# Where the bonus operand of a RWKV-7 head group is made, and in which order key, receptance and value streams run

## The chip, the cores and the metric

The kernel runs on one core of one Trainium2 chip. The metric is the device time of one execution in microseconds (us). The kernel before took 2336.88 us, the median of 3 runs (2333.94 to 2343.57). A change of over 0.5%, some 12 us, counts as faster or slower.

## The reference, cut to what matters

One encoder layer: a half-step SwiGLU FFN, a mixer, a second half-step FFN, each between RMS norms. The mixer projects the normed input once and splits the columns: eight dilated-attention heads (q, k, v) and eight RWKV-7 heads (r, k, v and three low-rank streams). RWKV-7 runs a delta-rule scan forward and backward, adds both, normalises per head, and adds a bonus:

```python
k_dir = k[:, :, None, :] * (1.0 + (a - 1.0) * k_a)          # one per direction d
...
y = ys[:, :, 0] + jnp.flip(ys[:, :, 1], axis=1)
y = ((y - mu) * lax.rsqrt(var + GN_EPS)).reshape(B, S, C) * lnx_w + lnx_b
bonus = jnp.einsum('bshn,bsdhn,hn->bsh', r, k_dir, r_k) / N_DIRS
y = y + (bonus[..., None] * v).reshape(B, S, C)
return y * g
```

All sizes here: 1024 tokens, width 1024, 8 + 8 heads of 64, FFN 2816, everything in float32, one layer.

## The kernel before, in words

Everything is traced once, in `run`, in five stages. The tile framework derives all waits. It also sets the order on each engine: program order is a priority, and an instruction that its plan holds ready is taken ahead of an earlier one that is not. On the chip each engine, and each DMA queue (SP's, ACT's, POOL's), then runs its list strictly in that order, so one late operand holds what is queued behind it.

- **FFN1** and the low-rank streams, which leave the in-context rates `a` of both directions in DRAM (`lr_d["a"]`, one 128x1024 tile for each of four pairs of heads; the backward one stored time-reversed).
- **Attention** (`attention`, heads h = 0 to 7). Beside head h one RWKV stream is projected (`project_rwkv`, L499): its weights are loaded on SP as eight 128x128 tiles `zraw`, split into two parts by ACT and VectorE (`zh`, `zl`, 16 buffers each, two streams' worth), and 48 matmuls of 128x512 on TensorE (L514) make 128 channels by 1024 tokens; `shift` (L521) mixes neighbours in time. Stream numbers: 0 to 3 are receptance (r), 4 to 7 key (k), 8 to 11 value (v), each for one pair of heads. Stream 0 is made before the attention; beside it run `streams = [4, 5, 6, 7, 1, 2, 3]` (L1269), none beside head 7. `stream` (L570) finishes them: an r stream is stored to `rk_d[ct]` (L580); a k stream is normalised (L586 to L602) and stored to `rk_d[4 + i]`, then for each direction the rate tile `ra` is turned into the directional key (`rb`, L610 ACT, L611 VectorE), stored to `ak_d[d][4 + i]`, and into `ra` times the normalised key (L613), stored to `ak_d[d][i]` (L614). These stores go through POOL's queue.
- **Scan entry.** `prep(n)` (L803) loads 128 tokens of rates, keys and receptance for both directions and forms the chunk matrices `lm`; `solve(n)` (L863) inverts them by 62 small dependent VectorE instructions (L879, L881) after a round trip of `X` through DRAM, ending with a transpose (L883). Between the two first of these the value streams are made: 8 and 9 after `prep(0)`/`solve(0)`, 10 and 11 after `prep(1)`/`solve(1)` (L1279 to L1282). A v stream is stored to `v_d` (L617), turned (L619 to L627) and written to `vt_d` on SP (L629).
- **Scan.** `merge(n)` and `chain(n)` for n = 0 to 7, with `prep(n + 3)` and `solve(n + 3)` issued behind `chain(n)`: three block buffers go round. The buffers of `merge` lie where the projection input `x` was, so it comes after the last value stream. `chain(0)` needs all four value streams, through `uv` and `sv` (L915).
- **Finish** (`finish_unit`, L982): eight units, each two pairs of heads by 256 tokens, with three sets of buffers. Each loads on SP the scan outputs `y0`, `y1`, the directional keys `k0`, `k1`, `r`, `v` (256 KB each) and `sg` (128 KB). POOL adds `y1` reversed to `y0` (L1001) and `k1` reversed to `k0` (L1004); VectorE multiplies by `r_k` and `r` (L1006, twice); TensorE centres y (L1002), sums squares (L1011), sums the bonus over a head (L1018), turns back the scale (L1021) and makes the gate (L1032); ACT and VectorE finish (L1003 to L1035, the gate product being L1033). Then `out_project` (L1093) adds the attention half `hp`, whose loads stand on SP behind those of all units, `post` adds the residual, and **FFN2** follows.

Of the kernel before, what the change touches and what calls it, by code (L numbers as in the profile page):

```python
# [10 lines left out]
F32 = mybir.dt.float32  # L11
F32R = mybir.dt.float32r
AF = mybir.ActivationFunctionType
OP = mybir.AluOpType
# [4 lines left out]
S, D, DFF, INW = 1024, 1024, 2816, 3456  # L19
# [144 lines left out]
class _Kernel:  # L164
# [334 lines left out]
    def project_rwkv(self, p, psum, x, blocks, wide=None):  # L499

        nc, V, A, T = self.nc, self.nc.vector, self.nc.scalar, self.nc.tensor
        for c0, n in blocks:
            for d in range(2) if 4 <= c0 < 8 else ():
                a = wide.tile([128, S], F32, name="ra", tag="ra")
                self.load(a, self.lr_d["a"][d][c0 - 4])
                self.rates.append(a)
            hl = self.columns(p, ATT + c0 * 128, n * 128)
            for ct in range(c0, c0 + n):
                cs = slice((ct - c0) * 128, (ct - c0 + 1) * 128)
                ps = [psum.tile([128, 512], F32, name="zr", tag="d", bufs=2) for half in range(2)]  # L510
                for half in range(2):
                    for k, (h, l) in enumerate(hl):
                        for i, (w, j) in enumerate(((h, 0), (h, 1), (l, 0))):
                            T.matmul(ps[half], w[:, cs], x[half][j][:, k, :], start=(k == 0 and i == 0),  # L514
                                     stop=(k == NK - 1 and i == 2))
# [54 lines left out]
    def stream(self, p, psum, ct, y):  # L570

        nc, V, A, G, T = self.nc, self.nc.vector, self.nc.scalar, self.nc.gpsimd, self.nc.tensor
        if ct == 12:
            A.activation(y, y, AF.Tanh)
        elif ct == 14:
            A.activation(y, y, AF.Tanh, scale=0.5)
            V.tensor_scalar(y, y, 0.5, 0.5, op0=OP.mult, op1=OP.add)
            self.nc.gpsimd.dma_start(self.sg_d, y)
        elif ct < 4:
            self.nc.gpsimd.dma_start(self.rk_d[ct], y)  # L580
        elif ct < 8:
            i = ct - 4
            sq = p.tile([128, S], F32, name="ksq", tag="u", bufs=1)
            kr = p.tile([128, S], F32, name="kr", tag="kr", bufs=1)
            g = self.kkc[:, i:i + 1]
            A.activation(sq, y, AF.Square, scale=g)  # L586

            vs = psum.tile([128, NT, 2], F32, name="kn", tag="t")
            for t in range(NT):
                T.matmul(vs[:, t, :], sq[:, t * 128:(t + 1) * 128], self.ones2[:, ::64], start=True, stop=True)  # L590
            rs = p.tile([128, 2 * NT], F32, name="krs", tag="krs")
            A.activation(rs, vs.rearrange("p a b -> p (a b)"), AF.Sqrt)
            V.tensor_scalar(rs, rs, 1e-12, None, op0=OP.max)
            V.reciprocal(rs, rs)
            A.activation(sq.rearrange("p (a c) -> p a c", c=64), rs[:, :, None].to_broadcast([128, 2 * NT, 64]), AF.Copy)
            for half in range(2):
                q = psum.tile([128, 512], F32, name="kt", tag="t")
                for t in range(4):
                    o = half * 512 + t * 128
                    T.transpose(q[:, t * 128:(t + 1) * 128], sq[:, o:o + 128], self.ident)  # L600
                o = slice(half * 512, half * 512 + 512)
                V.scalar_tensor_tensor(kr[:, o], y[:, o], g, q, op0=OP.mult, op1=OP.mult)  # L602
            self.nc.gpsimd.dma_start(self.rk_d[4 + i], kr)
            for d in range(2):
                a = self.rates.pop(0)
                turned = lambda z: z[:, ::-1] if d else z
                for half in range(2):
                    sl = slice(half * 512, half * 512 + 512)
                    b = p.tile([128, 512], F32, name="rb", tag="vts")
                    A.activation(b, a[:, sl], AF.Identity, scale=self.kah[:, i:i + 1], bias=self.ka1[:, i:i + 1])  # L610
                    V.tensor_tensor(b, b, turned(y)[:, sl], op=OP.mult)  # L611
                    self.nc.gpsimd.dma_start(self.ak_d[d][4 + i][:, sl], b)
                V.scalar_tensor_tensor(a, a, 1.0, turned(kr), op0=OP.add, op1=OP.mult)  # L613
                self.nc.gpsimd.dma_start(self.ak_d[d][i], a)  # L614
        else:
            i = ct - 8
            self.nc.gpsimd.dma_start(self.v_d[i], y)  # L617
            back = p.tile([128, S], F32, name="vrev", tag="us")
            V.tensor_copy(back, y[:, ::-1])  # L619
            for src, dst in ((y, self.vt_d[0]), (back, self.vt_d[1])):  # L620
                for g in range(2):
                    q = psum.tile([128, 4, 128], F32, name="vt", tag="t")
                    for j in range(4):
                        t = g * 4 + j
                        T.transpose(q[:, j, :], src[:, t * 128:(t + 1) * 128], self.ident)
                    vt = p.tile([128, 4, 2, 64], F32, name="vts", tag="vts")
                    A.activation(vt.rearrange("p a b c -> p a (b c)"), q, AF.Copy)  # L627
                    for par in range(2):
                        self.nc.sync.dma_start(dst[g * 512:(g + 1) * 512, par, i, :].rearrange("(j p) c -> p j c", p=128),  # L629
                                          vt[:, :, par])  # L630
# [351 lines left out]
    def finish_unit(self, p, psum, b, g, x, g2w):  # L982

        nc, V, A, G, T = self.nc, self.nc.vector, self.nc.scalar, self.nc.gpsimd, self.nc.tensor
# [2 lines left out]
        ps2, ts = slice(2 * g, 2 * g + 2), slice(b * FB, (b + 1) * FB)  # L987
        back = slice(S - (b + 1) * FB, S - b * FB)
        z = {}
        for nm, src, sl in (("y0", self.y_d[0], ts), ("y1", self.y_d[1], back), ("k0", self.ak_d[0][4:], ts),  # L990
                            ("k1", self.ak_d[1][4:], back), ("r", self.rk_d, ts), ("v", self.v_d, ts)):
            z[nm] = p.tile([128, 2, FB], F32, name="f_" + nm, tag="f_" + nm)
            self.load(z[nm], src[ps2, :, sl].rearrange("a p t -> p a t"))
        sg = p.tile([128, FB], F32, name="f_sg", tag="f_sg")
        self.load(sg, self.sg_d[:, ts])
        y, sq, k, v = z["y0"], z["y1"], z["k0"], z["v"]
        flat = lambda q: q.rearrange("p a t -> p (a t)")
        bank = lambda nm: psum.tile([128, 2, FB], F32, name=nm, tag="d")

# [1 line left out]
        G.tensor_tensor(y, y, z["y1"][:, :, ::-1], op=OP.add)  # L1001
        T.matmul(yc, self.cen, y, start=True, stop=True)  # L1002
        A.activation(sq, yc, AF.Square)  # L1003
        G.tensor_tensor(k, k, z["k1"][:, :, ::-1], op=OP.add)  # L1004
        for j in range(2):
            V.scalar_tensor_tensor(k[:, j, :], k[:, j, :], self.rkc[:, 2 * g + j:2 * g + j + 1], z["r"][:, j, :],  # L1006
                                   op0=OP.mult, op1=OP.mult)

        vs = psum.tile([128, 4, 2], F32, name="var", tag="d")
        for u in range(4):  # L1010
            T.matmul(vs[:, u, :], flat(sq)[:, u * 128:(u + 1) * 128], self.ones2[:, ::64], start=True, stop=True)  # L1011
# [12 lines left out]
        for j in range(2):  # L1024
            i = 2 * g + j
# [80 lines left out]
    def constants(self):  # L1106
# [19 lines left out]
        self.q_d, self.kt_d = self.dram("q", [4, 128, S]), self.dram("kt", [4, 128, S])  # L1126
        self.vt_d = self.dram("vt", [2, S, 2, 4, 64])
        self.ak_d = [self.dram(f"ak{d}", [8, 128, S]) for d in range(2)]
        self.y_d = [self.dram(f"y{d}", [4, 128, S]) for d in range(2)]
        self.x_d = [self.dram(f"x{j}", [64, 1024]) for j in range(4)]  # L1130

    def mix_columns(self):
# [10 lines left out]
        self.aog = self.column("attn_out_g", 4)  # L1143
        self.rkc = p.tile([128, 4], F32, name="rkc")
        nc.gpsimd.dma_start(self.rkc, io["rwkv_r_k"].rearrange("o (a b) c -> (b c) (o a)", b=2))
        self.w0h, self.a0h = p.tile([128, 2, 4], F32, name="w0h"), p.tile([128, 2, 4], F32, name="a0h")
        for t, nm in ((self.w0h, "rwkv_w0"), (self.a0h, "rwkv_a0")):
            nc.gpsimd.dma_start(t, io[nm].rearrange("o d (k p) -> p (o d) k", p=128))
# [25 lines left out]
    def run(self):  # L1174
# [4 lines left out]
        natural = list(range(NT))  # L1179
        with self.top as top:  # L1180

            self.pool(top, "edge", side="right").tile([128, 120], F32, name="edge")
            self.constants()
            s_xn = ExitStack()
            xp = self.pool(s_xn, "xn")
# [80 lines left out]
            self.load(self.bias12, self.io["k_bias12"])  # L1266
            NB, s_sr, s_pr, s_zr, s_pm = NC_ // BLK, ExitStack(), ExitStack(), ExitStack(), ExitStack()
            zr, pz = self.pool(s_zr, "zr", 2), self.pool(s_zr, "ps_r", 1, space=PSUM)
            streams, self.rates = [4, 5, 6, 7, 1, 2, 3], []  # L1269
            self.attention(pa, wa, lambda h: self.project_rwkv(zr, pz, x, [(ct, 1) for ct in streams[h:h + 1]], wa))  # L1270
            s_at.close()
            s_pa.close()
# [3 lines left out]
            R0, R1 = (self.pool(s_sr, f"blk{j}", 1, **R) for j in range(2))  # L1276
            self.scan_constants(sp)
            blk = {}
            for n, ct in ((0, 8), (1, 10)):  # L1279
                blk[n] = self.prep(n, sp, pp, (R0, R1)[n])  # L1280
                blk[n]["inv"] = self.solve(n, sp)
                self.project_rwkv(zr, pz, x, [(ct, 1), (ct + 1, 1)])  # L1282
            s_zr.close()
            s_xn.close()
            B0 = self.pool(s_sc, "blks", 1)
# [161 lines left out]
```

## Time and profile before

| | |
|---|---|
| profiled execution, whole | 2333.77 us |
| its span in the profile | 2332.0 us |
| TensorE matmul busy in the span | 2205.8 us (95%) |
| VectorE busy | 1763.1 us (76%) |
| ScalarE (ACT) busy | 1016.8 us (44%) |
| GpSimd (POOL) busy | 565.2 us (24%) |
| mean TensorE clock granted | 0.968 of full speed |

The profile is of one execution. A busy time is the sum of an engine's instruction spans; matmuls overlap each other, so a full TensorE column is not yet TensorE at its peak. In the view by windows each row has a stretch, its length, the busy time of PE (matmul), PEld (weight load), DVE (VectorE), ACT and POOL with the number of instructions, the granted clock, the share of the DMA engines in use and GB/s. In the timeline a row has start, length, engine, line, instruction, and in brackets the idle time ahead of it with what ended it. The stages by time: FFN1 and low rank to about 790, projection of q and k to 910, attention to 1190, scan entry to 1284, scan to 1559, finish to 1615, then output projection and FFN2 to the end.

### The profile page before, as it was taken

The numbers are of one execution on the slowest core, as the hardware profiler recorded it, in microseconds if no ns is written. First come the engines' busy times: TensorE is split into PE (matmuls) and PEld (weight loads), VectorE is DVE, ScalarE is ACT, GpSimd is POOL, SyncE is SP. The second block draws the span as 40 slices with busy tenths as digits, with TensorE's granted clock in tenths as the row PEclk, the third lists the DMA queues.
The fourth block names the chain that finished last, engine by engine and source line by source line (L and its number), as shares of the span: only waits on it lengthen the run. The fifth ranks groups of instructions, "written<-read, shape, count | busy, mean of one in ns | idle before, by whom it ended". The sixth has DMA issues, their size and how long they took to land. (4 is left out here: it accounts for less than half of the span.)

```text
span 2332.0 us, 41360 instructions
## 1 busy us (share of the span) xinstructions
PE 2205.8 (95%) x15556; PEld 1784.2 (77%) x15556; DVE 1763.1 (76%) x2862; ACT 1016.8 (44%) x1910; POOL 565.2 (24%) x682
## 2 busy tenths in 40 slices
PE   6999999999999998999998999988799999999997
PEld 4788888878877676778777777765578888887886
DVE  8899999975676254677668777737899999996565
ACT  4323333354577412667554554445443323235453
POOL 6243444410000010121111111122424453441000
PEclk8999999999999999999998899999899999999999
DMA  5245544486671514555257655368434454547655
GB/s 155 89 165 170 172 145 172 151 273 191 194 233 78 217 58 119 160 173 180 54 148 207 182 147 155 105 196 281 158 122 171 160 181 140 172 158 266 194 190 180
DMA packets 351965, 388.26 MB, mean 166 GB/s; under 512 B 73491, under 2 KB 256659, under 8 KB 351765
## 3 DMA queue, kind: packets, MB, share of 16 engines
q1 hardware_dynamic: 302048, 278.53, 39.3%
q0 software_dynamic: 29360, 94.44, 10.6%
q10 hardware_dynamic: 20356, 12.66, 1.8%
q8 instruction: 122, 2.00, 0.4%
q14 instruction: 79, 0.64, 0.1%
HBM read 260.68 MB, written 124.85 MB: 165 GB/s over the span
## 5 line engine op out<-in xcount | busy, mean ns | idle before, releaser
L186 ACT ACTIVATE wh<-raw 128x512 fp32r<-128x512 f32 (+1 forms) x273 | 167.9, 627 | 264.4 <-PE gu L81 97.5
L187 DVE TENSOR_TENSOR wl<-raw,wh 128x512 fp32r<-128x512 f32 (+1 forms) x273 | 278.5, 1023 | 5.2 <-ACT wh L186 4.3
L81 PE MATMUL gu<-xh,wh 128*128 128x512 f32 x704 | 277.1, 394 | 1.0 <-ACT xh L186 0.8
L81 PE MATMUL gu<-xl,wh 128*128 128x512 f32 x704 | 275.7, 392 | 0.0
L81 PE MATMUL gu<-xh,wl 128*128 128x512 f32 x704 | 275.7, 392 | 0.0
L415 PE MATMUL pd<-gl,gwh 128*128 128x512 f32 x616 | 240.4, 390 | 2.7 <-DVE gl L187 2.7
L415 PE MATMUL pd<-gh,gwh 128*128 128x512 f32 x616 | 239.5, 390 | 0.6 <-DVE row L86 0.6
L415 PE MATMUL pd<-gh,gwl 128*128 128x512 f32 x616 | 239.7, 389 | 0.0
L86 DVE TENSOR_TENSOR row<-gu,row 128x512 f32<-128x512 f32 x308 | 206.8, 684 | 24.6 <-PE gu L81 23.9
L187 DVE TENSOR_TENSOR gwl<-graw,gwh 128x512 fp32r<-128x512 f32 (+1 forms) x176 | 118.1, 674 | 128.7 <-ACT gwh L186 128.3
L116 POOL DMA_DIRECT2D d_hid<-row x154 | 84.7, 551 | 474.0 <-DVE row L114 451.1
L186 ACT ACTIVATE gwh<-graw 128x512 fp32r<-128x512 f32 (+1 forms) x176 | 101.2, 576 | 190.1 <-PE pd L415 157.4
L81 PEld LDWEIGHTS gu<-xh,wh 128*128 128x128 f32 x704 | 133.5, 190 | 30.0 <-ACT xh L186 2.0
L81 PEld LDWEIGHTS gu<-xl,wh 128*128 128x128 f32 x704 | 133.2, 189 | 27.4
L81 PEld LDWEIGHTS gu<-xh,wl 128*128 128x128 f32 x704 | 133.0, 189 | 27.5
L415 PEld LDWEIGHTS pd<-gl,gwh 128*128 128x128 f32 x616 | 115.6, 188 | 28.0 <-DVE gl L187 4.4
L415 PEld LDWEIGHTS pd<-gh,gwh 128*128 128x128 f32 x616 | 115.5, 188 | 25.6 <-DVE row L86 1.0
L415 PEld LDWEIGHTS pd<-gh,gwl 128*128 128x128 f32 x616 | 115.6, 188 | 23.7
L94 ACT ACTIVATE row<-row 128x512 f32<-128x512 f32 x44 | 27.8, 633 | 223.2 <-DVE row L86 215.6
L187 DVE TENSOR_TENSOR gl<-raw,gh 128x512 fp32r<-128x512 f32 x160 | 112.5, 715 | 15.1 <-ACT gh L186 14.9
L145 POOL TENSOR_TENSOR ws<-ws 128x512 f32<-128x512 f32 x88 | 114.3, 1299 | 1.2
L186 ACT ACTIVATE gh<-raw 128x512 fp32r<-128x512 f32 x160 | 98.0, 621 | 33.1 <-DMA raw<-in_ffn_w_down_dram 19.8
(356 smaller groups left out, 5251.5 us busy)
## 6 DMA issues: line engine op xcount, KB each, us to landing
d_hid<-row POOLq DMA_DIRECT2D x154, 256.0 KB, 2.4
graw<-d_hid SPq DMA_DIRECT2D x132, 256.0 KB, 3.1
raw<-in_ffn_w_gate_dram SPq DMA_DIRECT2D x88, 256.0 KB, 3.1
raw<-in_ffn_w_up_dram SPq DMA_DIRECT2D x88, 256.0 KB, 3.3
ws<-in_ffn_w_down_dram SPq DMA_DIRECT2D x88, 256.0 KB, 4.9
d_ws<-ws POOLq DMA_DIRECT2D x88, 256.0 KB, 2.3
raw<-d_ws SPq DMA_DIRECT2D x88, 256.0 KB, 2.7
raw<-in_ffn_w_down_dram SPq DMA_DIRECT2D x66, 256.0 KB, 3.5
```

The source lines that it names most:

```text
L81: self.K.nc.tensor.matmul(ps, a[:, k, :], b[:, k, :], start=(k == 0 and i == 0), stop=(k == 3 and i == 2))
L86: add = lambda o, x: V.tensor_tensor(o, ps, x, op=OP.add)
L94: A.activation(y[:, 0], y[:, 0], AF.Silu)
L116: put = lambda n, y: G.dma_start(self.hid[n - 1, j // 2], y)
L145: G.tensor_tensor(o, a, b, op=OP.subtract)
L186: self.nc.scalar.activation(h, src, AF.Copy)
L187: (eng or self.nc.vector).tensor_tensor(l, src, h, op=OP.subtract)
L415: T.matmul(ps[x], a[:, ts], b, start=(m == 0 and k == 0), stop=(m == NM - 1 and k == 2))
```

## The change

The bonus operand, `r_k * r * (k_dir0 + k_dir1)`, is made in `stream` at the end of each key stream, for all 1024 tokens of a pair of heads, and stored to a new DRAM tensor `fk_d`; `finish_unit` loads it as one tile. Since the sum of the two directional keys is `k * (k_a * (a0 + a1) / 2 + 2 * (1 - k_a / 2))` in the kernel's terms, it is made from the rate tiles: POOL adds them, ACT applies scale and bias with `r_k` folded in (`khr`, `k1r`, made once in `mix_columns`, kept in a padding tile that was there already), POOL multiplies r by k, VectorE multiplies both. For that a key stream loads the finished r stream from `rk_d`, so every k stream now comes after its r stream: `[4, 1, 5, 2, 6, 3, 7]`. Two more 128x1024 buffers (`rr`, `rs`) are taken. The four value streams all come after `solve(1)`.

```diff
         for c0, n in blocks:
-            for d in range(2) if 4 <= c0 < 8 else ():
-                a = wide.tile([128, S], F32, name="ra", tag="ra")
-                self.load(a, self.lr_d["a"][d][c0 - 4])
+            for tag, src in (("ra", self.lr_d["a"][0][c0 - 4]), ("ra", self.lr_d["a"][1][c0 - 4]),
+                             ("rr", self.rk_d[c0 - 4])) if 4 <= c0 < 8 else ():
+                a = wide.tile([128, S], F32, name=tag, tag=tag)
+                self.load(a, src)
                 self.rates.append(a)
+            if 4 <= c0 < 8:
+                self.rates.append(wide.tile([128, S], F32, name="rs", tag="rr"))
...
             self.nc.gpsimd.dma_start(self.rk_d[4 + i], kr)
-            for d in range(2):
-                a = self.rates.pop(0)
+            rates, r, both = self.rates[:2], *self.rates[2:]
+            self.rates.clear()
+            G.tensor_tensor(both, rates[0], rates[1][:, ::-1], op=OP.add)
+            G.tensor_tensor(r, r, y, op=OP.mult)
+            A.activation(both, both, AF.Identity, scale=self.khr[:, i:i + 1], bias=self.k1r[:, i:i + 1])
+            V.tensor_tensor(both, both, r, op=OP.mult)
+            self.nc.gpsimd.dma_start(self.fk_d[i], both)
+            for d, a in enumerate(rates):
...
-        for nm, src, sl in (("y0", self.y_d[0], ts), ("y1", self.y_d[1], back), ("k0", self.ak_d[0][4:], ts),
-                            ("k1", self.ak_d[1][4:], back), ("r", self.rk_d, ts), ("v", self.v_d, ts)):
+        for nm, src, sl in (("y0", self.y_d[0], ts), ("y1", self.y_d[1], back), ("k", self.fk_d, ts), ("v", self.v_d, ts)):
...
-        G.tensor_tensor(k, k, z["k1"][:, :, ::-1], op=OP.add)
-        for j in range(2):
-            V.scalar_tensor_tensor(k[:, j, :], k[:, j, :], self.rkc[:, 2 * g + j:2 * g + j + 1], z["r"][:, j, :],
-                                   op0=OP.mult, op1=OP.mult)
...
+        self.khr, self.k1r = self.edge[:, 0:4], self.edge[:, 4:8]
+        G.tensor_tensor(self.khr, self.kah, self.rkc, op=OP.mult)
+        G.tensor_tensor(self.k1r, self.ka1, self.rkc, op=OP.mult)
+        G.tensor_scalar(self.k1r, self.k1r, 2.0, None, op0=OP.mult)
...
-            streams, self.rates = [4, 5, 6, 7, 1, 2, 3], []
+            streams, self.rates = [4, 1, 5, 2, 6, 3, 7], []
...
-            for n, ct in ((0, 8), (1, 10)):
+            for n, cts in enumerate(([], [8, 9, 10, 11])):
                 blk[n] = self.prep(n, sp, pp, (R0, R1)[n])
                 blk[n]["inv"] = self.solve(n, sp)
-                self.project_rwkv(zr, pz, x, [(ct, 1), (ct + 1, 1)])
+                self.project_rwkv(zr, pz, x, [(ct, 1) for ct in cts])
```

More of the change, by code (lines that the diff above doesn't have):

```diff
@@ L995, in finish_unit @@
         self.load(sg, self.sg_d[:, ts])
-        y, sq, k, v = z["y0"], z["y1"], z["k0"], z["v"]
+        y, sq, k, v = z["y0"], z["y1"], z["k"], z["v"]
         flat = lambda q: q.rearrange("p a t -> p (a t)")
@@ L1128, in constants @@
         self.ak_d = [self.dram(f"ak{d}", [8, 128, S]) for d in range(2)]
+        self.fk_d = self.dram("fk", [4, 128, S])
         self.y_d = [self.dram(f"y{d}", [4, 128, S]) for d in range(2)]
@@ L1180, in run @@
         with self.top as top:
-            self.pool(top, "edge", side="right").tile([128, 120], F32, name="edge")
+            self.edge = self.pool(top, "edge", side="right").tile([128, 120], F32, name="edge")
             self.constants()
```

## The prediction

> **What bounds the kernel now.** I read the page first (which engine is full), then the view by windows over the stages that the change touches, then the waits, the chain and the timeline of the finish, last the timelines around the scan's entry. In the windows the columns behind the length are PE, PEld, DVE, ACT and POOL busy, clock, DMA share, GB/s.
>
> ```profile
> span 2332.0 us, 41360 instructions
> ```
>
> ```profile
> 940.00:1190.00 250.00, 246.66 (x2440) 197.05 (x2439) 168.29 (x448) 157.59 (x368) 47.66 (x61) 0.99 0.44 131
> 1190.00:1284.00 94.00, 83.60 (x765) 68.37 (x765) 75.97 (x207) 45.38 (x87) 12.64 (x27) 0.88 0.81 213
> 1284.00:1535.00 251.00, 230.86 (x4829) 194.31 (x4825) 177.94 (x526) 124.64 (x226) 36.90 (x69) 0.92 0.50 140
> 1535.00:1559.00 24.00, 18.94 (x347) 15.56 (x346) 4.78 (x8) 8.35 (x17) 8.78 (x8) 0.86 0.83 262
> 1559.00:1615.00 56.00, 47.30 (x192) 29.77 (x191) 41.51 (x70) 30.54 (x62) 15.12 (x12) 0.94 0.85 288
> 1615.00:1720.00 105.00, 85.89 (x409) 68.33 (x408) 87.41 (x123) 51.53 (x100) 26.53 (x18) 0.92 0.47 151
> ```
>
> The attention (first row) is TensorE's: 246.66 of 250 us, while POOL, ACT and DVE have room. The scan's entry (second row) has three full resources at once: PE 89%, DVE 81%, DMA 0.81. The finish (fifth row) is held by none of its engines alone: PE 84%, DVE 74%, DMA 0.85. What it waits for stands in the waits of 1558 to 1620 (total, times, longest) and in the chain:
>
> ```profile
> POOL f_y L1001 <- DMA f_y<-d_y: 18.3, 4, 7.2
> POOL f_k L1004 <- DMA f_k<-d_ak: 13.6, 5, 7.9
> ...
> DVE f_k L1006 <- POOL f_k L1004: 3.2, 2, 2.6
> ```
>
> ```profile
> 1582.14 4.06 DMA f_k<-d_ak
> ...
> 1591.08 6.07 DMA f_k<-d_ak
> ...
> 1597.30 1.28 POOL f_k L1004
> ```
>
> Twice the key loads stand on the chain that ended last, once with POOL's key sum behind them. Both go away with the change.
>
> **The change, part by part.**
>
> *Finish.* These rows are the operations removed, and the two that show the pace:
>
> ```profile
> L1006 DVE SCALAR_TENSOR_TENSOR f_k<-f_k,rkc,f_r x16: 445/480/1537, 1546.6 to 1604.3; 128x256 f32<-128x256 f32 x16
> ...
> L1004 POOL TENSOR_TENSOR f_k<-f_k,f_k x8: 1261/1267/1717, 1545.3 to 1602.4; 128x512 f32<-128x512 f32 x8
> ```
>
> ```profile
> f_k<-d_ak SPq DMA_DIRECT2D x16, 256.0 KB, 5.3
> ...
> f_r<-d_rk SPq DMA_DIRECT2D x8, 256.0 KB, 5.5
> ```
>
> ```profile
> L1033 DVE TENSOR_TENSOR f_y<-f_y,gate x8: 680/687/690, 1562.9 to 1613.4; 128x512 f32<-128x512 f32 x8
> ```
>
> ```profile
> 1560.76 1.02 PE L1002 MATMUL yc<-f_y,k_cen 128*128 128x512 f32 x2
> ...
> 1566.40 1.02 PE L1002 MATMUL yc<-f_y,k_cen 128*128 128x512 f32 x2
> ```
>
> Per unit go two VectorE instructions of 0.48 (0.96 us), one of POOL of 1.27, and three loads of 256 KB against one that comes. Over eight units that is 7.7 us of DVE, 10.1 of POOL and 16 x 256 KB = 4.2 MB, which at the window's 288 GB/s are 14.6 us of DMA. None of these adds up with the others; the pace tells what is gained. Now the gate product L1033 comes every (1613.4 - 1562.9) / 7 = 7.21 us. Two units that had all loads in time followed each other on PE in 1566.40 - 1560.76 = 5.64 us. **Upper end**: all seven gaps shrink to that, 7 x 1.57 = 11.0. **Lower end**: only the longest wait for POOL's sum goes, 2.6 us. DVE alone gives 7 x 0.96 = 6.7, as it is the engine in whose line the waits end. The y loads, which have the largest wait (18.3), remain, but come forward, because a third of the traffic around them is gone. I take **-7.5**, near DVE's share.
>
> What comes behind is late next: `out_project` waits for its `hp` rows, whose loads stand on SP behind those of the last unit, so it moves with the stage and I carry the gain over whole. If it does not (DVE is busy 87.41 of 105 us behind it), the gain is nothing; that is a rival.
>
> In the scan's last chain, TensorE is held by the first unit:
>
> ```profile
> 1544.65 1.22 PE L1002 MATMUL yc<-f_y,k_cen 128*128 128x512 f32 x1 [4.49 <-POOL f_y L1001]
> ```
>
> ```profile
> 1545.00:1550.00 5.00, 5.00 (x61) 3.50 (x61) 1.79 (x3) 1.08 (x2) 2.53 (x2) 0.50 1.03 335
> ```
>
> These are 4.5 us of waiting and some 2.5 more at a granted clock of 0.50. The y loads of the first unit stand ahead of its key loads on SP, so what is removed comes behind them. I cost this at nothing; at best it gains 7.0.
>
> *Attention.* A key stream adds two POOL instructions, one ACT, one DVE (all 128x1024), a load and a store of 512 KB. Nearest rows:
>
> ```profile
> L610 ACT ACTIVATE rb<-ra,ka,kah x16: 797/800/816, 928.9 to 1083.8; 128x512 f32<-128x512 f32 x16
> ```
>
> ```profile
> L613 DVE SCALAR_TENSOR_TENSOR ra<-ra,kr x8: 1215/1221/1224, 982.9 to 1088.7; 128x1024 f32<-128x1024 f32 x8
> ...
> L614 POOL DMA_DIRECT2D d_ak<-ra x8: 532/541/548, 984.4 to 1090.3; - x8
> ```
>
> ```profile
> L586 ACT ACTIVATE ksq<-us,c_rwkv_k_k x4: 1151/1151/1152, 970.2 to 1076.3; 128x1024 f32<-128x1024 f32 x4
> ```
>
> POOL: no row of this size; L1004 does half of it in 1.27, so 2.5 each (1.27 to twice the slowest, 3.4), 20 us for four streams. ACT: between L586's 1.15 and twice L610's 0.80, say 1.4, together 5.6. DVE: 1.2 as L613, together 4.9. All fit into what the first row leaves free (POOL 202, ACT 92, DVE 82 us), PE hides them, DMA is at 0.44. Cost nothing; if a head's softmax chain stood behind POOL's two instructions, at most 5 us in each of four heads, 20. On POOL's queue the directional-key stores and the head's own sums come behind the new ones, nobody else. The `rr` load stands on SP ahead of the weights: for stream 4 it waits for stream 0, made just before, 0 to 4 us at the start; I take 0. The three small instructions in `mix_columns` run on an idle POOL.
>
> Alternation puts a **key stream last**, and `prep(0)` needs its stores:
>
> ```profile
> 1172.58 0.59 POOL L580 DMA_DIRECT2D d_rk<-us  x1 [8.46 <-issue]
> ```
>
> ```profile
> 1192.82 0.50 SPq L182 DMA_DIRECT2D ka<-d_ak  x1
> ```
>
> ```profile
> DMA to landing us min/median/max: 2.3/2.5/2.8
> ```
>
> (The last row is that of the `rb` stores.) A key stream took 1090.3 - 1076.3 = 14.0 us from its square to its last store, plus 1.4 and 1.2 for the new ones in between, plus 2.5 to land. From 1172.6, where the last stream is done now, this ends at 1191.7; the load is issued at 1192.8. So the slack is one us. Bounds 0 and +5; I take **+1.5**.
>
> *Entry.* Value streams are the bulk of PE's work here, and `chain(0)` needs them all:
>
> ```profile
> L514 PE MATMUL zr<-xh,zl x61: 387/389/497, 1186.1 to 1255.4; 128*128 128x512 f32 x61
> ```
>
> ```profile
> 1238.11 0.29 DVE L881 TENSOR_TENSOR Ti<-Ti,ttmp 128x136 f32<-128x136 f32 x1
> 1238.32 0.29 DVE L187 TENSOR_TENSOR zl<-zraw,zh 128x128 fp32r<-128x128 f32 x1
> 1238.52 0.29 DVE L879 TENSOR_TENSOR ttmp<-X,Ti 128x128 f32<-128x128 f32 x1
> ```
>
> ```profile
> 1218.60 3.63 SPq L629 DMA_DIRECT2D d_vt<-vts  x3
> 1222.27 0.54 SPq L182 DMA_DIRECT2D kd<-d_ak  x1
> ```
>
> ```profile
> 1191.16 0.39 PE L514 MATMUL zr<-xh,zh 128*128 128x512 f32 x1
> 1191.38 0.39 PE L514 MATMUL zr<-xl,zh 128*128 128x512 f32 x1
> ```
>
> Today value splits slip in between two steps of a solve (second fence), so a lower place need not hold them up: I expect streams 8 and 9 where they are, 10 and 11 a little later, and `prep(1)` up to 3.6 us earlier, because stores of values no longer stand ahead of its `kd` load (third fence). Bounds: -4, and on the other side streams 10 and 11 running only after `solve(1)`, when TensorE has nothing else: 2 x 48 matmuls, one every 0.23 us (last fence), 22 us. I take **+1**, nearest to the row that shows the splits slipping in.
>
> **Sum**: -7.5 + 1.5 + 1 = -5, so 2333.77 - 5 = 2329 for an execution like the profiled one, which lies 3.1 under the median of 2336.88 of runs 9.6 apart. From the median the same sum gives 2332. I say **2330**.
>
> *A rule against it.* DVE and POOL disturb each other in this trace:
>
> ```profile
> 1550.11 1.54 DVE L1006 SCALAR_TENSOR_TENSOR f_k<-f_k,rkc,f_r 128x256 f32<-128x256 f32 x1
> ```
>
> ```profile
> 1550.10 1.27 POOL L1004 TENSOR_TENSOR f_k<-f_k,f_k 128x512 f32<-128x512 f32 x1 [0.16 <-DMA f_k<-d_ak]
> ```
>
> Beside POOL's sum the instruction took 1.54 instead of 0.45. The Trainium skill, "SBUF — State Buffer", section "Who interferes with whom", says that a VectorE instruction with two SBUF inputs and a GpSimd one that reads SBUF exclude each other for a whole instruction; the row agrees. By that rule each new POOL instruction can stop DVE for its length.
>
> **The rivals.**
>
> 1. *More than forecast.* The lighter burst also frees the last chain's 7.0 us, the finish reaches 5.64 a unit (-11.0), and `prep(1)`'s 3.6 count: 2333.8 - 11.0 - 7.0 - 3.6 + 1.5 = 2314 at most; with half of `prep(1)`'s part and 9.5 of the finish, **2317**. For it: DMA ran at 335 GB/s in that burst. Against: the held matmul waits for y, not k. 0.20.
> 2. *Slower: values starve.* DVE serves both solves before any split of streams 10 and 11, TensorE stands still, and `merge(0)` too, whose buffers wait for the last value matmul. It decides as soon as `solve(1)` has its X before stream 10 is split. Price 22: 2333.8 - 7.5 + 1.5 + 22 = **2350**; with one stream late, 2339. For it: DVE is 81% busy there, and the entry has no other bulk work for PE. Against: the slipping in. 0.16.
> 3. *The gain is absorbed* behind the finish, by the DVE work of 1615 to 1720: 2333.8 + 2.5 = **2336**. Against: the row loads of that stretch stand behind the units on SP. 0.09.
> 4. *POOL stops DVE* in the attention, 8 x 2.5 = 20 us, and heads wait: 2329 + 20 = **2349**. Against: 82 us of DVE are free there. 0.05.
>
> **How the numbers follow.** The forecast has 0.50, with a range of its own from 2321 to 2338. A measurement of this kernel tells 0.5%, 12 us, from no change, so faster means under 2325, slower over 2348.6. Faster: 0.18 of rival 1 and 0.10 of the forecast, 0.28. Slower: 0.09 of rival 2 and 0.03 of rival 4, 0.12. The rest, 0.60, is within. The range of 8 in 10 goes from 2314, the far end of rival 1, to 2347, which leaves out the worse halves of rivals 2 and 4.
>
> **What would show it.** Right: L1033 every 6 to 6.3 us, no wait for `f_k` on the chain, the last value matmul before 1260, `ka` issued by 1196, head intervals in the attention unchanged in sum. Wrong: a stretch between 1230 and 1290 in which PE has no `zr` matmul while L879 and L881 run back to back; a finish that still takes 7 us a unit because y is late; or a first load of `prep(0)` after 1198.

## The result, and the profile after

The changed kernel took 2325.51 us, the median of 20 runs (2318.77 to 2336.66), against 2335.56 of the kernel before (20 runs, 2328.55 to 2343.57). The ratio of the runs is 0.9965, 95% interval 0.9952 to 0.9977: 8.2 us faster (5.4 to 11.2), which is within the 0.5% that counts as no change; the two medians differ by 10.1. The forecast was 2330, from a sum of -5.

Of the profile after, first the span and the windows that the prediction showed of before. Columns behind the length: PE, PEld, DVE, ACT, POOL busy, clock, DMA share, GB/s.

```profile
span 2329.8 us, 41363 instructions
```

```profile
940.00:1190.00 250.00, 244.18 (x2353) 195.22 (x2350) 177.56 (x435) 158.01 (x365) 61.58 (x66) 0.97 0.48 142
1190.00:1284.00 94.00, 83.58 (x701) 66.81 (x701) 74.52 (x207) 41.55 (x88) 14.22 (x25) 0.88 0.72 193
1284.00:1535.00 251.00, 232.08 (x4818) 196.44 (x4817) 185.01 (x546) 129.93 (x231) 38.30 (x73) 0.91 0.55 151
1535.00:1559.00 24.00, 18.23 (x374) 15.09 (x370) 4.10 (x6) 7.31 (x16) 6.91 (x10) 0.86 0.75 226
1559.00:1615.00 56.00, 53.53 (x375) 37.94 (x376) 35.07 (x59) 35.28 (x71) 8.29 (x7) 0.97 0.79 265
1615.00:1720.00 105.00, 89.62 (x408) 71.88 (x407) 88.00 (x128) 52.43 (x101) 29.08 (x19) 0.89 0.42 138
```

These stretches are fixed in time, while the scan now ends 8.4 us later, so the fifth row holds some of the scan's last matmuls. The same three parts, cut at events, are fairer: first score to first load of `prep(0)` (attention), to the scan's last output copy (entry and scan), to the last gate-up matmul of FFN2. Before, then after:

```profile
932.50:1192.10 259.60, 256.26 (x2497) 204.81 (x2496) 171.08 (x457) 161.94 (x379) 48.82 (x64) 0.98 0.45 132
1192.10:1558.90 366.80, 331.20 (x5922) 276.51 (x5921) 257.38 (x735) 176.41 (x324) 57.16 (x101) 0.91 0.60 166
1558.90:2103.40 544.50, 516.68 (x2290) 415.39 (x2289) 497.18 (x593) 198.11 (x364) 214.72 (x231) 0.98 0.52 174
```

```profile
937.60:1204.66 267.06, 260.58 (x2511) 207.85 (x2510) 188.49 (x465) 166.91 (x388) 66.78 (x73) 0.97 0.48 143
1204.66:1567.30 362.64, 327.41 (x5912) 273.69 (x5911) 254.06 (x730) 175.77 (x319) 55.79 (x101) 0.90 0.60 165
1567.30:2100.80 533.50, 515.77 (x2286) 418.38 (x2285) 487.94 (x580) 199.05 (x364) 210.29 (x226) 0.97 0.51 172
```

The attention is 7.5 us longer. TensorE stands idle in it for 6.5 us instead of 3.3, and VectorE works 17.4 us more, where four instructions of 1.2 us were to come. The other 4.3 us are TensorE's busy time (260.58 against 256.26), at a granted clock of 0.97 instead of 0.98; an estimate that scales 256.26 by these two puts 2.6 of them down to the clock. Entry and scan are 4.2 shorter, with the same idle time of TensorE (35.2 against 35.6) and a clock no higher (0.90 against 0.91); why, these rows do not show. Over the executions below this part varies by more: 359.0 us at a clock of 0.93 in order_values, 384.6 at 0.87 in order_only (different orders of streams, but the clock differs too). Behind the scan 11.0 us are gained, nearly all of it TensorE's idle time (544.50 - 516.68 = 27.8 before, 533.50 - 515.77 = 17.7 after). The attention also begins 5.1 later, so the parts give 7.5 - 4.2 - 11.0 + 5.1 = -2.6, near the two spans' -2.2. The medians differ by more, because the profiled execution after (2331.59) lies 6.1 above its median and the one before 1.8 below that of the 20.

How the 11 us come about stands in the finish: the gate product by its line, the first row add of the output projection, and SP's timeline (the DMA issues of its queue, x6 for six in a row), after; then SP's before.

```profile
L1036 DVE TENSOR_TENSOR f_y<-f_y,gate x8: 677/687/690, 1570.3 to 1619.8; 128x512 f32<-128x512 f32 x8
...
L1105 DVE TENSOR_TENSOR row<-row,pw x16: 660/677/687, 1595.4 to 1657.9; 128x512 f32<-128x512 f32 x16
```

```profile
1584.56 0.46 SPq L182 DMA_DIRECT2D row<-d_hp  x1
...
1601.53 0.47 SPq L182 DMA_DIRECT2D row<-d_hp  x1
...
1605.80 3.63 SPq L182 DMA_DIRECT2D row<-d_hp  x6
```

```profile
1599.04 4.55 SPq L182 DMA_DIRECT2D row<-d_hp  x6
...
1615.99 0.90 SPq L182 DMA_DIRECT2D row<-d_hp  x2
```

The pace of the units is hardly changed: (1619.8 - 1570.3) / 7 = 7.07 us instead of 7.21. One execution says little about so small a difference: over the runs below the unit of before has a pace of 6.67 to 7.48 us (five kernels), the light one of 7.07 to 7.26 (six). But the first rows of the output projection are now loaded among the units' loads, and the first row add comes 28.1 us after the scan's end (1567.3), where it came 51.3 after it. So most of half 0 of the output projection is done inside the finish: 76 of its 96 matmuls and five of its eight row adds come before the last gate product, where it was 35 and two. From the scan's end to the last gate product TensorE is now 96% busy (before 84%; each row is one kernel's, from 1558.90 before, from 1567.30 after):

```profile
1558.90:1613.40 54.50, 45.80 (x185) 28.45 (x184) 40.07 (x67) 29.82 (x61) 15.12 (x12) 0.94 0.86 288
```

```profile
1567.30:1619.80 52.50, 50.15 (x223) 35.08 (x222) 39.00 (x64) 33.74 (x70) 8.28 (x7) 0.97 0.88 298
```

The wait for the key sum is gone, and that for y is longer than before (waits of 1558 to 1620; total, times, longest):

```profile
POOL f_y L1009 <- DMA f_y<-d_y: 29.9, 4, 18.7
```

### The profile page after: what moved, and what is told of

The parts are those of the page before. It is cut to its first block, busy times and chain, and to the rows that moved or that the text cites. A ratio compares the mean times of both kernels' runs of the same rounds, so it can differ in the third digit from the quotient of the medians.

```text
span 2329.8 us, 41363 instructions
## 1 busy us (share of the span) xinstructions
PE 2206.4 (95%) x15556; PEld 1787.0 (77%) x15556; DVE 1767.7 (76%) x2850; ACT 1022.4 (44%) x1914; POOL 580.1 (25%) x689
## 5 line engine op out<-in xcount | busy, mean ns | idle before, releaser
L187 DVE TENSOR_TENSOR wl<-raw,wh 128x512 fp32r<-128x512 f32 (+1 forms) x273 | 278.6, 1024 | 4.1 <-ACT wh L186 2.9
L187 DVE TENSOR_TENSOR gwl<-graw,gwh 128x512 fp32r<-128x512 f32 (+1 forms) x176 | 118.0, 673 | 130.1 <-ACT gwh L186 128.4
L187 DVE TENSOR_TENSOR gl<-raw,gh 128x512 fp32r<-128x512 f32 x160 | 112.3, 713 | 15.4 <-ACT gh L186 15.0
```

The lines of the kernel that those rows point to most:

```text
L187: (eng or self.nc.vector).tensor_tensor(l, src, h, op=OP.subtract)
```

## The experiments

Two theories. **T1**, the prediction's: a lighter unit runs faster, -7.5, and the rest costs next to nothing. **T2**, formed from the traces: the units keep their pace; the gain is half 0 of the output projection inside the finish, and it is larger, but the attention and the order of streams take some of it back. All ratios are to runs of the kernel before on the same chip; the third column is the ratio's distance from 1 in us of that kernel's median. The columns behind it come from one profiled execution each. "Attention" and "behind" are the first and third of the parts above; "d_x" is the time from the first load of `prep(0)` to the second set of `d_x` stores, which release `solve(1)`; "last zr" that to the last matmul of a value stream; "idle" TensorE's in entry and scan.

| kernel | ratio (95%) | us | attention | d_x | last zr | idle | behind |
|---|---|---|---|---|---|---|---|
| before | | | 259.6 | 45.5 | 63.3 | 35.6 | 544.5 |
| changed | 0.9965 (0.9952-0.9977) | -8.2 | 267.1 | 41.5 | 63.6 | 35.2 | 533.5 |
| fin_light | 0.9947 (0.9928-0.9967) | -12.4 | 258.8 | | | 38.6 | 533.8 |
| fin_loads | 0.9956 (0.9939-0.9973) | -10.3 | 257.8 | | | 37.9 | 534.6 |
| fin_ops | 0.9984 (0.9970-0.9998) | -3.7 | 258.0 | | | 37.3 | 540.4 |
| hp_early | 1.0036 (1.0019-1.0053) | +8.4 | 257.6 | | | 35.3 | 552.5 |
| order_only | 1.0050 (1.0030-1.0070) | +11.7 | 258.3 | 55.0 | 74.2 | 46.1 | 549.3 |
| values_only | 1.0005 (0.9987-1.0023) | +1.2 | 260.2 | 36.7 | 64.5 | 39.4 | 546.9 |
| order_values | 0.9982 (0.9963-1.0001) | -4.2 | 259.0 | 40.7 | 62.8 | 39.9 | 543.2 |
| order_vt_pool | 1.0005 (0.9992-1.0018) | +1.2 | 257.9 | 43.2 | 62.9 | 38.5 | 549.6 |
| bonus_order | 1.0023 (1.0002-1.0044) | +5.4 | 265.4 | 55.0 | 74.2 | 48.8 | 533.2 |
| rr_late | 0.9951 (0.9931-0.9971) | -11.5 | 263.0 | 42.8 | 64.8 | 35.2 | 534.1 |
| rr_late_dve | 0.9950 (0.9934-0.9967) | -11.7 | 261.2 | 40.6 | 61.7 | 37.3 | 532.1 |
| keep_order | 0.9979 (0.9966-0.9993) | -4.9 | 267.4 | 44.2 | 62.2 | 37.7 | 533.6 |

Without the bonus the attention takes 257.6 to 260.2 us in these executions, and with the heavy finish of before the part behind the scan 543.2 to 549.6 (hp_early aside): what is smaller than that is read from the ratios. TensorE's idle time in the attention spreads less: 2.9 to 3.5 us without the bonus, and with it 6.5 (changed), 6.9 (bonus_order), 5.9 (rr_late), 4.8 (rr_late_dve) and 7.7 (keep_order).

### The finish by itself

**fin_light**, in the kernel before:

```diff
         for nm, src, sl in (("y0", self.y_d[0], ts), ("y1", self.y_d[1], back), ("k0", self.ak_d[0][4:], ts),
-                            ("k1", self.ak_d[1][4:], back), ("r", self.rk_d, ts), ("v", self.v_d, ts)):
+                            ("v", self.v_d, ts)):
...
-        G.tensor_tensor(k, k, z["k1"][:, :, ::-1], op=OP.add)
-        for j in range(2):
-            V.scalar_tensor_tensor(k[:, j, :], k[:, j, :], self.rkc[:, 2 * g + j:2 * g + j + 1], z["r"][:, j, :],
-                                   op0=OP.mult, op1=OP.mult)
```

> The kernel before with the lighter finish alone: one key operand is loaded per unit, no second key, no r; POOL's key sum and both L1006 are left out. It leaves out the backward direction, r and r_k of the bonus. Nothing is added in the attention. Recorded reasons: the gate product every 6 to 6.3 us instead of 7.2, in all 7.5 us faster than before. Rival (the first half of the output projection is taken in among the units): the gate product still about every 7 us, the first row add some 15 us earlier against the end of the scan, from the end of the scan to the last gate-up matmul of FFN2 11 us less than the 544.5 of before, in all 9 to 13 us faster.

Measured: 12.4 us faster, the gate product every (1618.1 - 1567.3) / 7 = 7.26 us, first row add 29.5 after the scan's end instead of 51.3, 10.7 us less behind the scan. T2's numbers.

**fin_loads** has the first hunk alone, with `v` in place of `k1` and `r`; **fin_ops** the second alone.

> The kernel before with the finish's loads of the second key and of r left out, and its instructions kept: POOL adds v reversed and VectorE multiplies by v in their place, so the bonus is of other operands. Recorded reasons (pace set by VectorE's share of a unit): nothing of the 6.7 us comes, 0 to 3 faster. Rival (the row loads of the output projection come earlier on SP because 14 loads fewer stand ahead of them): most of the 11 us, 8 to 11 faster, first row add some 15 us earlier.

> The kernel before with the finish's key sum on POOL and both L1006 left out and all seven loads kept. It leaves out the backward direction, r and r_k of the bonus. Recorded reasons: most of the gain comes from VectorE's 0.96 us a unit, 5 to 7 us faster. Rival (SP's order decides): the row loads stay behind the units' loads, 0 to 4 us faster.

Measured: the loads alone bring 10.3 us, at the old pace of (1609.7 - 1559.5) / 7 = 7.17, with all of VectorE's and POOL's work in place; the instructions alone bring 3.7 (interval 0.5 to 7.0), and there the pace is (1606.7 - 1560.3) / 7 = 6.63, which over seven gaps is 4.1. The gate product and the first row add of fin_loads, then of fin_ops:

```profile
L1033 DVE TENSOR_TENSOR f_y<-f_y,gate x8: 648/686/689, 1559.5 to 1609.7; 128x512 f32<-128x512 f32 x8
...
L1102 DVE TENSOR_TENSOR row<-row,pw x16: 666/676/687, 1588.3 to 1652.3; 128x512 f32<-128x512 f32 x16
```

```profile
L1028 DVE TENSOR_TENSOR f_y<-f_y,gate x8: 681/686/689, 1560.3 to 1606.7; 128x512 f32<-128x512 f32 x8
...
L1097 DVE TENSOR_TENSOR row<-row,pw x16: 662/677/689, 1604.6 to 1652.5; 128x512 f32<-128x512 f32 x16
```

In fin_loads the row add comes 31.9 us after the scan's end (1556.4), in fin_ops it stays late, after 47.4 (1557.2). T1's mechanism may exist, then, at half its price and as long as the projection stays outside. But the profile does not prove it: order_values has the heavy unit of before and the same pace, 6.67. In fin_loads, too, less of the projection lies inside the finish than in the changed kernel (53 matmuls and four row adds before the last gate product; TensorE is busy for 45.72 of its 53.30 us, 86%), and yet the part behind the scan is 9.9 us shorter. So it is shown that the loads bring the gain; that it comes by way of the projection is read from the traces. A kernel with fewer loads and late rows, which would separate the two, was not run.

**hp_early** asks whether early rows are enough:

```diff
-            self.load(h2[t], self.hp_d[t * 128:(t + 1) * 128, :])
+            if half:
+                self.load(h2[t], self.hp_d[t * 128:(t + 1) * 128, :])
...
+            for t in self.order[:4]:
+                self.load(h2[t], self.hp_d[t * 128:(t + 1) * 128, :])
             self.finish_half(fi, pf, 1, x)
```

> The kernel before with the row loads of the output projection's first half written ahead of the second half of the finish, nothing else. SP then has the four row loads after the first unit's second load group, ahead of the loads of units 4 to 7. Recorded reasons (these loads follow the units and cost nothing themselves): no gain, or up to 5 us slower, since 2 MB go ahead of the units' loads. Rival (half 0 of the output projection waits for nothing but its rows): first row add 15 us or more earlier, 8 to 13 us faster than before with the finish as heavy as ever.

Neither: 8.4 us slower, and T2 in this form falls. In hp_early the same two lines read:

```profile
L1033 DVE TENSOR_TENSOR f_y<-f_y,gate x8: 677/686/689, 1555.1 to 1613.4; 128x512 f32<-128x512 f32 x8
...
L1103 DVE TENSOR_TENSOR row<-row,pw x16: 630/679/689, 1585.3 to 1651.2; 128x512 f32<-128x512 f32 x16
```

The row add comes early (34.2 after the scan's end), but the units take 8.33 us each on the mean, 7 x 1.12 = 7.8 more in all. Most of that is one gap of 14.4 us, from the fourth gate product (1577.0) to the fifth (1591.4), whose unit's loads the four row loads stand ahead of. Early rows by themselves do not pay; in the kernels where they do, the units have 16 loads (4.2 MB) fewer, and the changed kernel brings two rows forward, not four.

### The order of streams and the place of the value streams

```diff
-            streams, self.rates = [4, 5, 6, 7, 1, 2, 3], []
+            streams, self.rates = [4, 1, 5, 2, 6, 3, 7], []
```

is **order_only**; **values_only** is the change's last hunk alone; **bonus_order** is the changed kernel with 8, 9 and 10, 11 where they were.

> The kernel before with the stream order 4 1 5 2 6 3 7 alone; bonus and value streams as before. Recorded reasons: a key stream last ends about 1191, so `ka` of the first prep(0) is issued 0 to 5 us later (1193 to 1198) and the whole is 0 to 5 us slower, 1.5 likely. Rival, in which the 12 us by which the changed kernel enters the scan later come from the load of r ahead of the weights: the first zr matmul of stream 4 stays at 933, ka as above. Rival, in which they come from the order: ka at 1200 to 1206 and the whole 8 to 15 slower.

> The kernel before with all four value streams placed behind solve(1) alone. Recorded reasons: between 4 us faster and 22 slower, +1 likely; last value matmul 1254 to 1260. Rival: the entry costs 3 to 5 us more (the changed kernel's first solve step came 15.7 later and the first chain instruction 18 later, where its first prep load came 12.5 later), and the scan gives most of it back: 0 to 4 us in the whole.

> The changed kernel with value streams 8 and 9 behind solve(0) and 10 and 11 behind solve(1) again, as before. Recorded reasons: the finish gains 7.5 and the attention gives up 1.5, so 6 us faster than before, 1 us faster than the changed kernel. Rival (the gain comes from the output projection's first half being taken in among the units, and most of the cost lies in the attention): finish and attention as in the changed kernel, 8 to 12 us faster than before.

The order alone costs 11.7 us (interval 7.0 to 16.4; the medians differ by 8.0), the value streams alone nothing that can be told (+1.2, interval -3.0 to +5.4), and the changed kernel without its last hunk is 5.4 slower than before instead of 8.2 faster. For order_only and bonus_order none of the recorded readings held as a whole: the first load came early and the kernel was slower all the same, and bonus_order was to be 6 to 12 us faster. The key stream being last is not why: in order_only the first load of `prep(0)` is issued at 1191.27, earlier than the 1192.10 of before. What changes comes behind it on SP. In the kernel before, in order_only, then in order_values:

```profile
1199.90 0.50 SPq L182 DMA_DIRECT2D ka<-d_ak  x1
...
1209.31 0.93 SPq L629 DMA_DIRECT2D d_vt<-vts  x2
```

```profile
1203.17 0.79 SPq L182 DMA_DIRECT2D th_w<-d_w  x1
1206.19 6.41 SPq L629 DMA_DIRECT2D d_vt<-vts  x4
1212.65 0.54 SPq L182 DMA_DIRECT2D ka<-d_ak  x1
```

```profile
1199.59 4.44 SPq L182 DMA_DIRECT2D ka<-d_ak  x2
1204.09 0.50 SPq L629 DMA_DIRECT2D d_vt<-vts  x1
1205.47 0.36 SPq L182 DMA_DIRECT2D kd<-d_ak  x1
```

In order_only eight stores of value stream 8 stand ahead of `ka` of `prep(1)`, and the last four hold SP for 6.4 us; before, that load was issued at 1199.90, ahead of them all. The `d_x` stores of `solve(1)` come after 55.0 us instead of 45.5, the last value matmul after 74.2 instead of 63.3, and TensorE is idle for 46.1 us of entry and scan instead of 35.6. bonus_order has the same three numbers (55.0, 74.2, 48.8). Two runs test that.

**order_values** has both moves, no bonus. **order_vt_pool** is order_only with

```diff
-                        self.nc.sync.dma_start(dst[g * 512:(g + 1) * 512, par, i, :].rearrange("(j p) c -> p j c", p=128),
+                        self.nc.gpsimd.dma_start(dst[g * 512:(g + 1) * 512, par, i, :].rearrange("(j p) c -> p j c", p=128),
```

> The kernel before with both moves and without the bonus: stream order 4 1 5 2 6 3 7, and all value streams behind solve(1). If the two moves only add up (12 for the order, 0 for the values, as measured alone): 10 to 14 us slower than before. If they belong together (with the alternating order the stores of value stream 8 stand on SP ahead of the loads of prep(1); behind solve(1) they come after them): 0 to 4 us slower, the second set of d_x stores within 38 to 42 us of the first load of prep(0), against 55.0 with the order alone and 45.5 before.

> The kernel before with the stream order 4 1 5 2 6 3 7 and the value stores d_vt issued on POOL's queue instead of SP's. If the 12 us of the order come from those stores standing on SP ahead of the loads of prep(1): the second set of d_x stores within 46 us of the first load of prep(0) instead of 55.0, and 0 to 4 us slower than before. If they come from the key stream being last, or from what the value streams take of VectorE and TensorE: still 8 to 14 us slower.

Either cures most or all of it: -4.2 (interval -8.6 to +0.2) and +1.2 (-1.9 to +4.2) instead of +11.7, `d_x` after 40.7 and 43.2, last value matmul after 62.8 and 62.9, and TensorE's idle time 39.9 and 38.5 instead of 46.1. The two moves do not add up; the place of the value streams is the repair of what the order does to SP's queue. Whether order_values is a little faster than before is open: its interval takes in 1.

### The attention

**rr_late** loads r behind the weights of its key stream:

```diff
-                             ("rr", self.rk_d[c0 - 4])) if 4 <= c0 < 8 else ():
...
             hl = self.columns(p, ATT + c0 * 128, n * 128)
+            if 4 <= c0 < 8:
+                self.rates += [wide.tile([128, S], F32, name=q, tag="rr") for q in ("rr", "rs")]
+                self.load(self.rates[2], self.rk_d[c0 - 4])
```

> The changed kernel with the load of r placed behind the eight weight loads of its key stream instead of ahead of them. Recorded reasons (the load of r costs nothing): same time as the changed kernel within 2 us. Rival (SP stands behind that load at the head of the attention): the first zr matmul of stream 4 goes from 946.8 back to 933 to 936, the first load of prep(0) from 1204.7 to 1192 to 1197, and the whole is 4 to 10 us faster than the changed kernel, 12 to 18 faster than before.

Inconclusive. The first zr matmul is back beside the first score (931.1 and 930.3), and prep(0) is loaded 263.0 us behind the latter instead of 267.1. But the interval of its ratio overlaps that of the changed kernel, TensorE's idle time in the attention is nearly the same (5.9 against 6.5), and the rest of the difference is busy time of the same 2511 matmuls, 257.07 us at a granted clock of 0.99 against 260.58 at 0.97:

```profile
930.30:1193.31 263.01, 257.07 (x2511) 205.10 (x2510) 189.03 (x465) 167.26 (x386) 66.97 (x73) 0.99 0.49 146
```

The wait that was to go is still there. In both kernels it stands ahead of the two `ra` loads, not of `rr`. SP's waits and issues at the head of the attention, changed kernel and rr_late:

```profile
SPq L182 <- DMA d_rk<-us: 9.6, 1, 9.6
```

```profile
920.16 1.10 SPq L182 DMA_DIRECT2D kp<-d_kt  x2
930.98 0.80 SPq L182 DMA_DIRECT2D ra<-d_a  x2
931.83 0.43 SPq L182 DMA_DIRECT2D rr<-d_rk  x1
```

```profile
SPq L182 <- DMA d_rk<-us: 9.4, 1, 9.4
```

```profile
913.13 1.11 SPq L182 DMA_DIRECT2D kp<-d_kt  x2
923.73 0.80 SPq L182 DMA_DIRECT2D ra<-d_a  x2
924.58 1.85 SPq L182 DMA_DIRECT2D zraw<-in_w_in_dram  x4
```

Every kernel here that loads r for stream 4 has this wait, and no other has it. Why it stands ahead of `ra`, I have not found, so what it costs by itself was not measured. The same kernels are those that take the buffers `rr` and `rs`, so a wait for the place of a buffer is as possible as one for r; neither was tested.

VectorE shows a second cost. The changed kernel, one moment of VectorE and of POOL:

```profile
977.72 0.68 DVE L653 TENSOR_TENSOR sb<-s,n 128x512 f32<-128x512 f32 x1
978.32 2.56 DVE L620 TENSOR_TENSOR rb<-rb,us 128x512 f32<-128x512 f32 x1
980.80 1.21 DVE L612 TENSOR_TENSOR rs<-rs,rr 128x1024 f32<-128x1024 f32 x1
```

```profile
977.93 2.40 POOL L610 TENSOR_TENSOR rr<-rr,us 128x1024 f32<-128x1024 f32 x1 [6.29 <-ACT e L722]
```

`rb`, normally 0.68 us, ends 0.55 after POOL's product ends (980.88 against 980.33): it did not get through until that product was done. **rr_late_dve** puts both POOL instructions on VectorE:

```diff
-            G.tensor_tensor(both, rates[0], rates[1][:, ::-1], op=OP.add)
-            G.tensor_tensor(r, r, y, op=OP.mult)
+            V.tensor_tensor(both, rates[0], rates[1][:, ::-1], op=OP.add)
+            V.tensor_tensor(r, r, y, op=OP.mult)
```

> The changed kernel with r loaded behind the weights, and the two POOL instructions of the bonus (sum of the rates, r times k) on VectorE. If the attention's 4 to 8 us come from POOL stopping VectorE: rb (L620) back from 1.17 to 0.68 us, the weight split L187 from 0.39 to 0.31, VectorE's work in the attention 186 us against 189.0 in spite of 9.8 us taken over, first score to first load of prep(0) 259 to 261 us against 263.0, and the whole 2 to 4 us faster than with POOL. If they come from the traffic, or from what the key stream asks of VectorE itself: VectorE's work above 195, the stretch 263 us or longer, the whole not faster.

VectorE, by line and form, in rr_late and then in rr_late_dve (busy us, mean ns):

```profile
L187 DVE TENSOR_TENSOR zl<-zraw,zh 128x128 fp32r<-128x128 f32 x78 | 28.2, 390 | 6.7 <-ACT zh L186 6.0 <-ACT n L669 0.3 <-PE zr L517 0.2
L620 DVE TENSOR_TENSOR rb<-rb,us 128x512 f32<-128x512 f32 x16 | 18.5, 1173 | 0.3 <-ACT rb L619 0.2
```

```profile
L187 DVE TENSOR_TENSOR zl<-zraw,zh 128x128 fp32r<-128x128 f32 x78 | 25.3, 348 | 6.6 <-ACT zh L186 6.5
L620 DVE TENSOR_TENSOR rb<-rb,us 128x512 f32<-128x512 f32 x16 | 10.9, 684 | 0.0
```

VectorE does 9.8 us more of its own and is busy for 186.8 us instead of 189.0; the attention is 1.8 us shorter (261.2, just beyond the 259 to 261 expected; the weight split L187 comes back to 0.35 us, not to 0.31), and TensorE's idle time in it 4.8 instead of 5.9. That is somewhat less than half of the 4.0 between rr_late and order_values (259.0), which has the same order and no bonus. In the whole, where 2 to 4 us were expected, it is not to be told from rr_late.

**keep_order** makes the bonus without moving any stream: a key stream stores k times both directions to a new tensor, and the r stream that comes later loads it and multiplies.

```diff
+            if c0 in (1, 2, 3, 4):
+                self.rates.append(wide.tile([128, S], F32, name="rr", tag="rr"))
+                self.load(self.rates[-1], self.ks_d[c0] if c0 < 4 else self.rk_d[0])
...
+            if ct:
+                ks = self.rates.pop()
+                G.tensor_tensor(ks, ks, y, op=OP.mult)
+                self.nc.gpsimd.dma_start(self.fk_d[ct], ks)
...
```

> The bonus made beside the attention with the order of streams and the place of the value streams as before: a key stream stores k times both directions, the later r stream of the same heads loads it, multiplies on POOL and stores the bonus operand; only stream 4 loads the r that is there, behind its weights. If the attention's cost is that of the order (a key stream last, values later): the finish's 11 us remain whole, 9 to 12 us faster than before, first load of prep(0) at 1190 to 1194. If it is that of the bonus instructions and their traffic themselves: first load of prep(0) 4 us or more later against the first score than the 259.6 of before, and 4 to 8 us faster.

4.9 us faster, attention 267.4: the second theory. The finish's gain is whole (533.6 behind the scan), entry and scan are as before, and the attention is 7.8 us longer although no stream was moved, with 4.3 us more idle time of TensorE (7.7 against 3.3). For three of the four key streams it stores one operand more than the changed kernel does (k times both directions, 512 KB), so the two costs need not be equal.

## Why the prediction was right, and where it was not

- **Time and class** were right: 2330 forecast, 2325.5 measured, within 0.5%. The sum of -5 compares with the measured -8.2, and that it came so near was luck in good part: a gain that was too small (-7.5 for 11.0) stood beside a cost of the attention that was put at nothing.
- **Finish, -7.5**: sign right, mechanism wrong. The step that failed is "I take -7.5, near DVE's share", with the pace of 6 to 6.3 us a unit that it implied. The changed kernel has 7.07, and y comes late, which were two of the signs of being wrong. VectorE's and POOL's share alone gave 3.7 (fin_ops, 0.5 to 7.0), the loads alone 10.3 (fin_loads). The premise under it failed too: "`out_project` waits for its `hp` rows, whose loads stand on SP behind those of the last unit". That order is no constant of the kernel. It is planned anew from what else there is to load, and with fewer loads two rows go among the units. What I had called the upper end, 11.0, was reached, but not by the shorter unit that stood behind it.
- **The last chain's stall, cost 0**: nothing came of it; TensorE still waits for POOL's sum of y at the first unit, and y still arrives late.
- **Attention, cost nothing**: undersized. The idle time on VectorE and POOL was there, yet the stage lengthened by 7.5 us in the changed kernel's profile, 5.8 in bonus_order, 3.4 in rr_late, 7.8 in keep_order, at clocks of 0.97 to 0.99; TensorE's idle time in it grew by 3.1, 3.5, 2.6 and 4.3. Rival 4 had the mechanism and put 20 us on it; VectorE was in fact busy for some 12.5 more than its own new work (17.4 less the 4.9 of L612), and taking POOL out shortened the stage by 1.8. "For stream 4 it waits for stream 0 ... I take 0" was wrong as to the wait: it is 9.6 us of SP, ahead of `ra` and not of `rr`, with an end of 4 in the prediction.
- **Last key stream, +1.5**: 0. The first load of `prep(0)` comes within 1.5 us of the attention's last reduction (1190.7 and 1192.10 before, 1191.9 and 1191.27 in order_only), with the key stream last or not. The slack of one us that I had worked out was not on the path.
- **Entry, +1**: right in size (TensorE's idle time in entry and scan 35.2 against 35.6), for a reason that I had not seen. "Streams 8 and 9 where they are" holds (last value matmul 63.6 us behind the first load, 63.3 before), `prep(1)` comes 4 us earlier, as hoped. But without the last hunk the new order would have cost some 12 us, by value stores ahead of `prep(1)` on SP: the rival that was missing. Rival 2, value streams starved by both solves, did not occur.

The profile's signs: no wait for the key sum was right, though the chain that ended last goes back to 1628.64 only and so does not show the finish. The attention's length, which was to stay, grew by 7.5 us. `ka` at 1196, the first load of `prep(0)` by 1198 and the last value matmul by 1260 failed (1205.24, 1204.66, 1268.3), all three by the attention's later start and greater length and not by the entry.

## What to carry to other kernels

When loads are taken out of a stage, ask what the planner will put in their place: the gain here came without a faster unit, with TensorE less idle and most of the next stage's first half done inside the finish, and loading that work early without making the room first lost 8.4 us. Where a queue is shared, read what the new order of producers puts ahead of the next consumer's loads, since two moves that cost 12 and 0 us alone may be free together. Idle time on VectorE does not pay for new POOL work beside it: count the stops of VectorE as well, and read a stage's cost from idle time, which moved less than the stage's length did with the clock.

## What the runs showed of the hardware

A 128x1024 product of two operands took 2.39 us on POOL (L610) and 1.22 on VectorE (rr_late_dve); I had estimated 2.5 for POOL from a row half its size. A VectorE instruction with two operands in SBUF that started 0.39 us behind POOL's product ended only 0.55 us after it (2.56 us instead of 0.68). The Trainium skill, "SBUF — State Buffer", section "Who interferes with whom", says that a VectorE instruction with two SBUF inputs contends with a GpSimd one that reads SBUF, and this row agrees. The sixteen 128x512 products of a kernel became 1.17 instead of 0.68 on the mean by it, while TensorE stood idle for only 3.1 us more in the whole attention.

What stays open: the wait for the r store ahead of `ra`, the rest of the attention's cost, whether the lighter finish gains by its smaller traffic itself or only by the rows that come early, and whether rr_late_dve (0.9950, interval 0.9934 to 0.9967) beats the changed kernel (0.9952 to 0.9977); the intervals overlap.
